# An attention layer's gate projection, moved behind the attention loop and done with seven block products for each pair of heads

## The chip, the cores and the metric

The kernel runs on one core of a Trainium2 chip. A core has TensorE (PE in the profile; its weight loads are PEld), VectorE (DVE), ScalarE (ACT), GpSimd (POOL) and SyncE (SP, which only issues DMAs here), an SBUF of 128 partitions, and a PSUM of eight banks into which TensorE accumulates. The metric is the device time of one execution in microseconds, the median of several runs.

## The reference

A trunk of two layers over 1024 latent tokens of width 1024, with a context prefix of 256 tokens. The first layer, which the change is about, is windowed attention with a gate:

```python
proj = h_lat @ w_in                                  # (1024, 1024) @ (1024, 5120)
q = apply_rope(split_heads(proj[..., :q_end], 16), cos, sin)       # 16 heads of 128
k = apply_rope(split_heads(proj[..., q_end:k_end], 4), cos, sin)   # 4 key heads
v = split_heads(proj[..., k_end:v_end], 4)
z = proj[..., v_end:]                                # the gate, 2048 wide
kv_c = h_ctx @ w_in[:, q_end:v_end]                  # keys, values of the context
...
o = windowed_attention(q, k, v, kc, vc, sink)        # |i-j| <= 128, all context keys, a sink logit
y = (o * jax.nn.silu(z)) @ w_out
...
x = x + gate * y
```

The second layer is a Conformer convolution with its own gate and output projection, and a final RMSNorm ends it. `h_lat` is the modulated norm of `x`. Everything is float32.

## The kernel before

**Products in three parts.** Each float32 operand of a product is split into a high part (rounded to TensorE's fp32r) and a low part (the rest). A product of 128x128 weights with 512 tokens is three matmuls: high by high, high by low, low by high (`mm3`, `gemm_half`). ScalarE makes the high part by a copy, VectorE or GpSimd the low part by a subtraction (`split_lo`). `Hh` and `Hl` are the high and low parts of `h_lat`, transposed: eight tiles of 128 channels by 1024 tokens.

**Stages.** The start computes the modulation, transposes `x` and projects the first key head, query head and value head. Then comes the attention loop over 128 steps `(h, qb)`: 16 heads, 8 blocks of 128 queries. Then the output projection (`proj_attn`), the convolution's input projection and convolution, and its output projection.

**A step of the attention loop.** `scores` issues six matmuls for the next step's queries against up to 384 window keys and 256 context keys; VectorE subtracts the mask and takes the maximum into `p_page`, ScalarE takes the exponent, VectorE the reciprocal, GpSimd scales. `transposes` turns the probabilities of this step (five 128x128 blocks) into PSUM, from which ScalarE makes `pthi` and VectorE `ptlo`. After four blocks `pv` multiplies them with V, multiplies by the gate and writes `ozd` in DRAM. Scores and transposes share a PSUM pair (`ps_s`, two buffers of two banks).

**Fill.** Between these TensorE works through `fillq`, a queue of projection jobs: `job(("q", n))` and `job(("z", n))`, 48 matmuls of 128x512 each. `fill(FILL)` takes twelve matmuls per step. The gate job ends in `finish`: `silu(z)` is formed as z(tanh(z/2)+1)/2 and stays in `zt` until `pv`. Every fourth head a new key head begins; its K and V jobs run in one piece between two steps.

**Other work in the loop.** `ada_rest` sums the modulation of the second layer row by row on VectorE (one call per step, accumulator in `mask_page`). `low_parts` splits the output weights of both layers once and puts the low halves into DRAM (`wolA`, `wolC`). In the last head the first seven rows of blocks of the output projection run early as fill (`early_proj`, EARLY_ROWS).

**Order.** `pin("P")` keeps TensorE's instructions in the order of the program; on the other engines and in SyncE's queue a scheduler orders them when the program is built. `after(...)` puts an operation behind the softmax's on its engine. SBUF beside the constants is 45 pages of 4 KB per partition (`pg`) and 6 half pages (`hp`); a page is handed out in the order in which pages were freed, and a write to it waits for the last reader.

## Time and profile before

| | |
|---|---|
| time, median of 3 runs | 1757.66 us (1756.83 to 1758.03) |
| profiled execution: span of its instructions | 1752.9 us |
| profiled execution: time of its own beside the span | none given by the page |
| attention loop, 110 to 850 us: VectorE, ScalarE, GpSimd busy | 416.1, 360.1, 403.4 us of 740 |
| HBM read, written | 188.70 MB, 41.69 MB |

The page lists each engine's busy time, the span in 40 slices, the chain of work that ended last, and groups of instructions. A group's line reads: source line, engine, operation, output<-inputs by the program's names, shapes, count, then busy time in us and the mean of one in ns, then the engine's idle time before them and what ended it. All instructions are issued through one helper, so that the source line is the same for all; groups are told apart by their tile names: `psg<-hh_page,whi_page` is a projection, `pss<-ident,p_page` the transposes, `p_page<-pss,mask_page,nsink` the masked maximum, `mask_page<-wsum_raw,...` and `dww_raw` the modulation sum, `wlo_page` a weight's low part, `low_page` the output weights' low halves. Matmuls overlap: a matmul's own duration is longer than the distance to the next.

### The profile page before, as it was taken

Reading aid. Unit: us, or ns where it says so; the run is one execution under the profiler, and the core shown is the slowest. Engines: PE = TensorE matmul, PEld = TensorE weight load, DVE = VectorE, ACT = ScalarE, POOL = GpSimd, SP = SyncE. Lnnn points to the kernel's source line nnn. Section 1 sums busy time; section 2 is a strip of 40 time slices with the busy share of each in tenths; the row PEclk is TensorE's granted clock in tenths of the full one; section 3 lists DMA queues with packets and bytes.
Section 4 is the critical chain, followed back from the end, with each engine's and each line's share of the span. In section 5 each row is a group of like instructions: output and inputs, shape, how many; then the busy total and the mean of one; then the engine's idle time right before and its main releaser. Section 6 shows DMA issues by size and latency. Waiting matters only on the chain.

```text
span 1752.9 us, 23877 instructions
## 1 busy us (share of the span) xinstructions
PE 1720.7 (98%) x8420; PEld 1424.8 (81%) x8420; DVE 1148.3 (66%) x2079; ACT 889.4 (51%) x1548; POOL 895.4 (51%) x705
## 2 busy tenths in 40 slices
PE   7999999999999999999999999999999999999997
PEld 4788888888888888888888888888888888788886
DVE  6755564556546563656315189999999999867823
ACT  7555553445345444545334355554665564466731
POOL 0245654566636565653101267998898888130300
PEclk9999999999999999999999999999999999999999
DMA  9334443444334542436777733011121202377971
GB/s 313 107 82 139 136 133 85 145 147 145 100 105 143 152 142 87 136 119 203 279 250 239 241 90 105 13 54 31 43 79 36 91 30 79 120 254 243 325 264 48
DMA packets 195324, 242.45 MB, mean 138 GB/s; under 512 B 11798, under 2 KB 126790, under 8 KB 195204
## 3 DMA queue, kind: packets, MB, share of 16 engines
q1 hardware_dynamic: 188516, 230.10, 40.3%
q10 hardware_dynamic: 6688, 10.83, 2.6%
q8 instruction: 66, 1.08, 0.3%
q14 instruction: 54, 0.44, 0.1%
HBM read 188.70 MB, written 41.69 MB: 131 GB/s over the span
## 4 chain that ended last, share of the span: by engine, by line
PE 86%; DMA 5%; DVE 3%; POOL 2%; ACT 2%; issue 2%; SPq 1%; ACTq 0%; POOLq 0%; DVEq 0%
PE psg L89 44%; PE pss L89 22%; PE pso L89 19%; DMA araw_page<-in_ada_w_dram 1%; POOL rope_half L89 1%; DMA low_page<-in_conv_w_out_dram 1%; DMA rope_half<-rope_half 1%; SPq L89 1%; DMA low_page<-in_attn_w_out_dram 1%; DMA wolC<-low_page 1%; DVE mask_page L89 1%; ACT p_page L89 0%; POOL wlo_page L89 0%; POOL low_page L89 0%; DMA wraw_page<-in_attn_w_in_dram 0%
## 5 line engine op out<-in xcount | busy, mean ns | idle before, releaser
L89 POOL TENSOR_TENSOR odd_half<-odd_half,prod_half 128x513 f32<-128x513 f32 (+2 forms) x252 | 312.8, 1250 | 24.2 <-ACT prod_half L89 11.0
L89 PE MATMUL psg<-hh_page,whi_page 128*128 128x512 f32 x600 | 237.6, 396 | 0.0
L89 PE MATMUL psg<-hh_page,wlo_page 128*128 128x512 f32 x600 | 236.9, 395 | 0.0
L89 PE MATMUL psg<-hl_page,whi_page 128*128 128x512 f32 x600 | 236.8, 395 | 0.0
L89 POOL TENSOR_TENSOR wlo_page<-wraw_page,whi_page 128x1024 fp32r<-128x1024 f32 x70 | 173.1, 2475 | 104.1 <-ACT whi_page L89 83.2
L89 ACT ACTIVATE prod_half<-ubuf,dww 128x513 f32<-128x513 f32 (+2 forms) x252 | 165.1, 674 | 107.3 <-POOL odd_half L89 105.1
L89 POOL TENSOR_SCALAR p_page<-p_page,sc 128x640 f32<-128x640 f32 (+1 forms) x128 | 100.8, 787 | 224.4 <-DVE sc L89 208.7
L89 PE MATMUL psg<-h2h_page,whi_page 128*128 128x512 f32 x464 | 183.9, 396 | 0.0
L89 PE MATMUL psg<-h2h_page,wlo_page 128*128 128x512 f32 x464 | 183.0, 394 | 0.0
L89 PE MATMUL psg<-h2l_page,whi_page 128*128 128x512 f32 x464 | 182.4, 393 | 0.0
L89 DVE SCALAR_TENSOR_TENSOR pss<-ubuf,dww,pss 128x512 f32<-128x512 f32 (+3 forms) x270 | 172.3, 670 | 0.1
L89 DVE SCALAR_TENSOR_TENSOR pss<-ubuf,wsum,pss 128x512 f32<-128x512 f32 (+3 forms) x270 | 171.7, 670 | 0.2
L89 DVE TENSOR_TENSOR ptlo<-pss,pthi 128x640 fp32r<-128x640 f32 (+1 forms) x144 | 103.3, 717 | 64.0 <-ACT pthi L89 62.8
L89 ACT ACTIVATE p_page<-p_page,sc 128x641 f32<-128x641 f32 (+1 forms) x128 | 102.7, 802 | 74.1 <-DVE sc L89 69.7
L89 ACT ACTIVATE pthi<-pss 128x640 fp32r<-128x640 f32 (+1 forms) x144 | 88.6, 615 | 91.7 <-PE pss L89 86.3
L89 PEld LDWEIGHTS psg<-hh_page,wlo_page 128*128 128x128 f32 x600 | 112.9, 188 | 26.3
L89 PEld LDWEIGHTS psg<-hh_page,whi_page 128*128 128x128 f32 x600 | 113.0, 188 | 20.8 <-DVE kvc_page L89 0.2
L89 PEld LDWEIGHTS psg<-hl_page,whi_page 128*128 128x128 f32 x600 | 112.9, 188 | 20.7
L89 ACT ACTIVATE whi_page<-wraw_page 128x1024 fp32r<-128x1024 f32 x88 | 92.6, 1053 | 69.0 <-PE psg L89 25.5
L89 PE MATMUL pso<-h2l_page,whi_page 128*128 128x512 f32 x304 | 119.9, 394 | 0.0
L89 PE MATMUL pso<-h2h_page,whi_page 128*128 128x512 f32 x304 | 119.8, 394 | 0.0
L89 PE MATMUL pso<-h2h_page,wlo_page 128*128 128x512 f32 x304 | 119.6, 394 | 0.0
(244 smaller groups left out, 4105.2 us busy)
## 6 DMA issues: line engine op xcount, KB each, us to landing
wraw_page<-in_conv_w_in_dram SPq DMA_DIRECT2D x48, 512.0 KB
wraw_page<-in_attn_w_in_dram SPq DMA_DIRECT2D x40, 512.0 KB
wol_page<-wolA SPq DMA_DIRECT2D x32, 512.0 KB
wo_page<-in_attn_w_out_dram SPq DMA_DIRECT2D x32, 512.0 KB
wo_page<-in_conv_w_out_dram SPq DMA_DIRECT2D x32, 512.0 KB
wol_page<-wolC SPq DMA_DIRECT2D x32, 512.0 KB
rope_half<-rope_half ACTq DMA_DIRECT2D x80, 128.0 KB
araw_page<-in_ada_w_dram SPq DMA_DIRECT2D x32, 256.0 KB
```

What stands on the lines that cost most here:

```text
L89: r = f(*a, **k)
```

## The change

Two heads' gate weights and the two halves of the tokens make a 2x2 by 2x2 block product over the two halves of the 1024 channels. The change computes it with seven block products in place of eight (Winograd's form). `t_prep` forms the four sums of activation blocks, a quarter of the channels in each of the heads 0, 4, 8 and 12, and stores them split in DRAM (`td`); `z_prep` forms the sums of weight blocks for each pair; `dense` issues the products and `z_evac` combines them. `pv` no longer gates: it stores the attention output in DRAM (`od`), and `z_out` reads it back, multiplies by the gate and writes `ozd`. The first pairs are fill of the last three heads, the others run behind the loop. Scores are issued two steps ahead, fill is five matmuls before the transposes and four or five behind them, K and V of the next key head are fill jobs that read the context's operands back from DRAM (`kept`), the early rows of the output projection are gone, and its low weight halves are made on GpSimd when needed (`wolA` is gone).

```diff
-FILL = 12
-EARLY_ROWS = 7
-EARLY_FROM = 3
...
+        after_q[h] = [("q", h + 2)] if h + 2 < NH else []
+        if g < NG and h % 4 == 1:
+            after_q[h].append(("k", g))
+        if g < NG and h % 4 == 3:
+            after_q[h].insert(0, ("v", g))
...
-        items = [... for w, d in ((Wo, wolA), (Wp, wolC)) for m in range(2) for kk in range(NK)]
+        items = [... for w, d in ((Wp, wolC),) for m in range(2) for kk in range(NK)]
...
+            split_lo(G, wl, w, wh)
...
-        stt(oz[:, 0:512], o, 0.5, zt[h][:, sl], ALU.mult, ALU.mult)
-        SY.dma_start(out=ozd[h, :, sl], in_=oz[:, 0:512])
+        act(oz[:, 0:512], o, AF.Copy)
+        SY.dma_start(out=od[h, :, half * 512:half * 512 + 512], in_=oz[:, 0:512])
...
+    def t_prep(k):
...
+        def v(out, p, q, op):
+            after(tt(V, out, p, q, op))
+        def g(out, p, q, op):
+            after(tt(G, out, p, q, op), anchor_p)
+        def out(n, t):
+            q = pg.alloc(F32R, [2, 512], "tq")
+            act(q[:, 0], t, AF.Copy)
+            after(split_lo(V, q[:, 1], t, q[:, 0]))
+            SY.dma_start(out=td[n, k], in_=low(q))
+            pg.free(q)
+        g(c, l11, l12, ALU.subtract)
+        v(a, h11, h12, ALU.subtract)
+        yield
+        v(a, a, c, ALU.add)
+        out(0, a)
...
+    def z_prep(g):
+        r1, r2 = zraw.pop(g)
+        z_pair(g, 0, r1, V)
+        yield
+        tt(G, s3, r1[:, 0:4], r2[:, 0:4], ALU.add)
+        tt(G, r2[:, 0:4], r2[:, 0:4], r2[:, 4:8], ALU.add)
+        yield
+        tt(G, r1[:, 0:4], r1[:, 0:4], r2[:, 0:4], ALU.add)
+        tt(G, r1[:, 4:8], r1[:, 4:8], r1[:, 0:4], ALU.add)
+        yield
+        z_pair(g, 1, r1, V)
...
+        z_pair(g, 2, r2, G)
...
+    PRODS = {"p1": (0, 0, "11"), "p2": (0, 4, "21"), "r6": (1, 0, "t2"), "p3": (1, 4, "22"),
+             "r5": (2, 0, "t1"), "r4": (2, 4, "t4"), "r7": (3, 0, "t3")}
...
+        if alone[0]:
+            t = s_alloc() if name == "p2" else c
+            act(t, c, AF.Silu)
+            tt(G, t, t, o, ALU.mult)
...
+                for k in range(4):
+                    rh, rl = xq(mv, k)
+                    for m, (w, x) in enumerate(((wh, rh), (wh, rl), (wl, rh))):
+                        PE.matmul(o, w[:, k0 + k], x, ...)
+                        yield
...
+        if tgen:
+            next(tgen, None)
+        if h >= NH - 3:
+            next(pgen, None)
+        elif lstate[0] == "open" or h % 4 == 0 and len(pg.free_) > 3:
             lstate[0] = next(lows, "shut")
...
-            scores(*nxt)
-            fill(15 if h and h % 4 == 0 and qb < 4 else FILL)
+            scores(*steps[i + 2])
+        fill(5)
         if pvq:
             pv(*pvq.popleft())
         transposes(h, qb)
+        fill(4 + qb % 2)
...
+    alone[0] = True
+    for v in zall:
+        if v == "starve":
+            next(pgen)
+        elif v is not None:
+            next(pgen, None)
+            next(pgen, None)
+            next(adag, None)
+            lstate[0] = next(lows, "shut")
```

## The prediction

> **What bounds the kernel now.** I read the head of the page and its slices first, to see which engine is full and where.

> ```profile
> span 1752.9 us, 23877 instructions
> PE 1720.7 (98%) x8420; PEld 1424.8 (81%) x8420; DVE 1148.3 (66%) x2079; ACT 889.4 (51%) x1548; POOL 895.4 (51%) x705
> ...
> PE   7999999999999999999999999999999999999997
> ...
> PEclk9999999999999999999999999999999999999999
> ```

> TensorE is busy in every slice but the first and the last, at full clock. A busy digit does not say that it is at its peak, so I looked next at the chain that ended last, for the distance between matmuls, and at TensorE's list of waits between 105 and 850 us, which is the attention loop.

> ```profile
> 292.41 3.47 PE pso L89 x21
> ...
> 977.41 44.47 PE pss L89 x192
> ...
> engine line waited for: us in total, times, longest us
> PE pss L89 <- DVE ptlo L89: 3.6, 2, 3.2
> PE pss L89 <- DVE sc L89: 1.3, 3, 0.9
> PE psg L89 <- DVE rope_half L89: 1.0, 1, 1.0
> PE pss L89 <- POOL p_page L89: 0.5, 1, 0.5
> ```

> 192 matmuls of 128x512 in 44.47 us are 0.2316 us each, without a gap. The loop of some 740 us holds only 3.6 + 1.3 + 1.0 + 0.5 = 6.4 us of waits. So this kernel is bound by the number of matmul columns, and any matmul taken out is worth its full 0.2316 us, as long as the other engines keep up.

> **What the change removes from TensorE.** Before, the gate projection is 16 heads x 2 halves x 24 matmuls = 768. After, each of 8 pairs has seven products of 4 x 3 matmuls: 8 x 84 = 672. The 96 that go are worth 96 x 0.2316 = **-22.2 us**. Nothing else changes in number: the Q, K, V, score, transpose, P·V and output matmuls are the same, and the 84 early output matmuls that filled the last head only move behind the loop, at the same price each. In the order of the built program two pairs (168 matmuls) run as fill in the last heads and six (504) alone behind the loop.

> The waits of the old loop belong to its order (scores one step ahead, K and V run in one piece between groups). With scores two steps ahead they go: **-6.4 us**; I charge the new order's own waits below.

> **The shorter step.** Fill per step falls from 12 to 9.5 matmuls (five, then four or five). The timeline of TensorE shows one old step:

> ```profile
> 396.45 0.40 PE L89 MATMUL psg<-hh_page,whi_page 128*128 128x512 f32 x1
> ...
> 399.26 0.71 PE L89 MATMUL pss<-ident,p_page 128*128 128x128 f32 x5
> 399.73 0.42 PE L89 MATMUL pss<-kh_page,qh_page 128*128 128x384 f32 x1
> ...
> 400.70 0.39 PE L89 MATMUL psg<-hh_page,whi_page 128*128 128x512 f32 x1
> ```

> Twelve fills take 2.81 us, five transposes 0.47, six score matmuls 0.97: 4.25 us. The new step is 4.25 - 2.5 x 0.2316 = 3.67 us; every fourth one also has the P·V block of 3.47 us. Four steps come to 3 x 3.67 + 7.14 = 18.2 us. That is still TensorE work, but the other engines now have to serve a step in 3.67 us where they had 4.25. So I listed what they do per step, between 280 and 840 us, VectorE's groups first, then GpSimd's and ScalarE's:

> ```profile
> L89 DVE CUSTOM_DVE_ANT_0 p_page<-pss,mask_page,nsink 128x640 f32<-128x640 f32 x72 | 63.1, 876 | 10.5 <-PE pss L89 10.1
> L89 DVE TENSOR_TENSOR ptlo<-pss,pthi 128x640 fp32r<-128x640 f32 x69 | 56.6, 820 | 31.4 <-ACT pthi L89 31.4
> L89 DVE SCALAR_TENSOR_TENSOR mask_page<-wsum_raw,cs,mask_page 128x256 f32<-128x256 f32 x47 | 38.3, 814 | 0.0
> L89 DVE TENSOR_TENSOR rope_half<-psg,cos_page 128x512 f32<-128x512 f32 x26 | 18.0, 691 | 32.0 <-ACT rope_half L89 24.9 <-POOL ql_page L89 5.8 <-issue 0.7
> L89 DVE RECIPROCAL sc<-sc 128x1 f32<-128x1 f32 x94 | 15.0, 160 | 64.0 <-ACT p_page L89 63.8
> L89 DVE TENSOR_TENSOR ozl_page<-ozf_page,ozh_page 128x1024 fp32r<-128x1024 f32 x6 | 7.3, 1223 | 4.7 <-ACT ozh_page L89 4.7
> ...
> L89 POOL TENSOR_TENSOR low_page<-low_page,lhi_half 128x512 f32<-128x512 f32 x50 | 65.4, 1308 | 0.0
> L89 POOL TENSOR_TENSOR wlo_page<-wraw_page,whi_page 128x1024 fp32r<-128x1024 f32 x26 | 63.5, 2445 | 20.1 <-ACT whi_page L89 19.1 <-POOL p_page L89 1.0
> L89 POOL TENSOR_SCALAR p_page<-p_page,sc 128x640 f32<-128x640 f32 x71 | 57.9, 815 | 116.0 <-DVE sc L89 109.0 <-DMA wol_page<-wolA 3.0 <-PE psg L89 2.9
> ...
> L89 ACT ACTIVATE p_page<-p_page,sc 128x641 f32<-128x641 f32 x71 | 58.8, 829 | 52.5 <-DVE sc L89 52.3
> L89 ACT ACTIVATE pthi<-pss 128x640 fp32r<-128x640 f32 x70 | 48.9, 698 | 48.7 <-PE pss L89 48.5
> ```

> A plain step costs VectorE 0.88 + 0.82 + 0.16 + 0.81 (the modulation sum, one per step) + a quarter of 0.69 (one half of Q's rotation every four steps) = 2.84 us, of 3.67. ScalarE has 0.83 + 0.70 for the softmax. Plain steps fit, and I charge **+1 us** for the occasional late one (the old loop paid 6.4 us over 128 steps).

> **The added preparation on VectorE.** In heads 0, 4, 8 and 12 each of ten steps also gets a piece of the preparation of the activation sums (t_prep): 11 VectorE operations on 128x512 and 5 on GpSimd for each of four tiles, in the same heads in which the low halves of the convolution's output weights go over GpSimd. Whether that fits hangs on one thing that the trace shows: a VectorE operation with both inputs in SBUF does not run beside a GpSimd one. The modulation sum's durations (minimum, median, maximum), and the two engines side by side:

> ```profile
> L89 DVE SCALAR_TENSOR_TENSOR mask_page<-wsum_raw,cs,mask_page x47: 472/485/2203, 304.0 to 824.6; 128x256 f32<-128x256 f32 x47
> ...
> 395.83 0.49 DVE L89 SCALAR_TENSOR_TENSOR mask_page<-dww_raw,cs,mask_page 128x256 f32<-128x256 f32 x1
> ...
> 398.79 2.10 DVE L89 SCALAR_TENSOR_TENSOR mask_page<-wsum_raw,cs,mask_page 128x256 f32<-128x256 f32 x1
> 400.82 0.15 DVE L89 RECIPROCAL sc<-sc 128x1 f32<-128x1 f32 x1
> 400.89 0.80 DVE L89 TENSOR_TENSOR ptlo<-pss,pthi 128x640 fp32r<-128x640 f32 x1
> ...
> 395.97 1.03 POOL L89 TENSOR_SCALAR p_page<-p_page,sc 128x640 f32<-128x640 f32 x1 [5.41 <-DVE sc L89]
> 396.96 1.30 POOL L89 TENSOR_TENSOR low_page<-low_page,lhi_half 128x512 f32<-128x512 f32 x1
> 398.21 2.40 POOL L89 TENSOR_TENSOR wlo_page<-wraw_page,whi_page 128x1024 fp32r<-128x1024 f32 x1
> ```

> The same sum takes 0.49 us alone and 2.10 us when it meets the weight split on GpSimd, and it ends 0.28 us after that split; the softmax split behind it starts late. In the mean it takes 0.814 us, 0.33 us of it waiting. [...]

> One t_prep operation I take at 0.69 us (the rotation's 128x512 row, the nearest in size) plus the wait. VectorE's step is then 2.51 us free (2.84 - 0.33) + 1.1 x 0.69 = 3.27 us, plus the wait on 2.1 operations. At the old mean of 0.33 us that is 3.96 us: four steps are 15.9 of TensorE's 18.2, but each of the three steps without P·V is 0.3 us too long. There is slack for that: from one transposes to the next TensorE has 3.67 - 0.47 = 3.2 us of other work, and the high and low split between them need 0.70 + 0.82, which leaves 1.7 us. So 0 us. The wait should be longer, though: in such a head of 36.4 us GpSimd has six rotation operations, five of t_prep and some five low halves of 1.31 us and one split of 2.45, 24 us, or 0.65 of the time, and a VectorE operation that meets one waits 0.9 us of it in the mean (half of 1.31 or more): 0.6 us. Then the step is 4.53 us, three steps are 2.6 us too long, and the P·V step gives that back to VectorE but not to TensorE. Over 10 such triples (4 tiles x 2.5) it is 26 us without the slack, and 10 x (2.6 - 1.7) = 9 us with it. Ends 0 and +26; I take **+9**.

> **The last head.** In the built order three steps of head 15 have no fill at all, since the second pair's operands are not yet issued. Such a step has 0.47 + 0.97 = 1.44 us for TensorE, and cannot be shorter than transposes, high split and low split in a row, 0.47 + 0.70 + 0.82 = 2.0 us and hops. Three times 0.7, and a wait for the second pair's product: **+3** (0 to 8: a weight split of 2.45 and an addition chain of 4 x 1.31 on GpSimd late by one step).

> **The stage behind the loop.** 6 x 84 matmuls and the rest of the second pair, some 560 x 0.2316 = 130 us. GpSimd has per pair 4 additions, 1 sum and 4 gate products of 1.31 us and a split of 2.45: 14.2 us of TensorE's 19.5; with 9 leftover low halves (11.8) and the first output-weight splits (4 x 2.45) it is 107 us. If every two-input VectorE operation (per pair two splits of 1.22, one of 0.69, seven sums of 0.49: 6.6 us) pushes it back, 146 us, which is 16 late. Pairs are prepared more than one ahead, and gate products may run late without TensorE noticing. Ends 0 and +16; **+4**.

> **The handover and the rest.** The output projection's low weight split moves from a DRAM copy (wolA) to GpSimd: 2.45 us per 24 matmuls of 5.56 us, beside TensorE. Cover is the pair before; if the first split is late it costs its 1.06 + 2.45 us. **+1** (0 to 4). The copies that go (wolA) and come (od, td, kept) stay off the path: TensorE did not wait for a DMA in the old loop. The convolution starts earlier, otherwise unchanged: 0.

> **Sum.** -22.2 - 6.4 + 1 + 9 + 3 + 4 + 1 = -10.6 us. The page gives no time of its own for the profiled execution beside its span of 1752.9 us; the runs' median is 1757.66, 4.8 us outside the span, which I keep. 1757.66 - 10.6 = **1747 us**.

> **Rivals.**
> *All of it is covered.* The waits turn out as in the old loop, with 2 us in all: 1757.66 - 28.6 + 2 = 1731. For it: VectorE's 15.9 us of 18.2. [...] Chance 0.24.
> [...] VectorE's steps in heads 0, 4, 8, 12 cost TensorE, and GpSimd, held out by VectorE, delays the pairs behind the loop. It decides from 28.6 us of stalls on; without the slack a mean wait of 0.45 us is enough, 30 x (3.27 + 2.1 x 0.45 - 3.67) = 16 us in the loop beside 8 behind it and the 5 of the rest. Upper ends: 26 + 16 + 1 + 3 + 1 = 47. Midway to the break-even point, 38: 1757.66 - 28.6 + 38 = 1767. For it: the rows above; against: GpSimd is 51% busy. Chance 0.25.
> *The pairs arrive late.* [...] Chance 0.09.
> That the change does not do what it says is not open: the built program has the 672 matmuls.

> **Numbers.** Forecast 1747, chance 0.42, itself from 1739 to 1755. What a measurement can tell from no change is 0.2%, 3.5 us: below 1754.1 is faster. Faster: 0.24 + 0.39 + 0.02 = 0.65. Same: 0.03 of the forecast, 0.05 of the late pairs, 0.02 of the lock: 0.10. Slower: 0.25. The range of 8 in 10 goes from 1731 (all covered) to 1769 (just past the lock's middle).

> **What would show it.** In the profile after, TensorE's list of waits between 105 us and the end of the loop should hold 10 to 16 us, most of it for ptlo and sc (VectorE) in heads 0, 4, 8 and 12; the preparation's operations (tx_page) should have a minimum near 0.69 us and a mean over 1; the stage behind the loop should last 130 to 136 us, with waits for zlo or zhi at pair borders. It is wrong if TensorE's matmul distance changes, if a DMA ends its waits, or if the waits sum to under 5 or over 30 us.

## The result and the profile after

| | before | after |
|---|---|---|
| time, median | 1757.24 us (1755.0 to 1758.03, 4 runs) | 1806.13 us (1801.96 to 1807.98, 4 runs) |
| span of the profiled execution | 1752.9 us | 1804.3 us |
| mean granted clock of TensorE | 0.996 | 0.986 |

The change makes the kernel slower by 2.8% (ratio 1.028, 95% interval 1.0264 to 1.0296). The forecast was 1747 us, faster, with a range up to 1769.

The head of the page after, with the slices of TensorE:

```profile
span 1804.3 us, 24082 instructions
...
PE 1723.9 (96%) x8324; PEld 1413.5 (78%) x8324; DVE 1228.5 (68%) x2120; ACT 917.1 (51%) x1597; POOL 1048.8 (58%) x784
...
PE   7989998999999998889899999999999999999997
```

TensorE has the 96 matmuls less that were counted (8420 before, 8324 now), but slices with 8 (each is 45 us) stand at the start of the loop, at 271 us, where head 4 begins, at the loop's end, in the new stage and at its border to the output projection. The starts of the transposes (minimum, median and maximum duration, then first and last start) give the loop's ends, before and after; the output projection's matmuls give the end of the new stage:

```profile
L89 PE MATMUL pss<-ident,p_page x608: 269/273/328, 110.4 to 849.0; 128*128 128x128 f32 x152
```

```profile
L86 PE MATMUL pss<-ident,p_page x608: 270/272/447, 111.6 to 719.2; 128*128 128x128 f32 x152
...
L86 PE MATMUL psg<-woh_page,ozh_page x96: 387/394/793, 880.3 to 1025.5; 128*128 128x512 f32 x96
```

Below, "the loop" is the time from the first to the last of these transposes (after: 719.2 - 111.6 = 607.6 us), "the stage" the time from there to the first output matmul (161.1 us). "Lost time" adds up, over all matmuls of a part, how much longer the distance to the next start was than it usually is for that matmul between the same neighbours; it holds the waits and the stretches at half clock (a granted clock of 0.50).

| part | lost before | lost after | difference |
|---|---|---|---|
| loop | 14.8 | 50.3 | +35.5 |
| stage behind it | - | 23.4 | +23.4 |
| output projection | 1.3 | 10.3 | +9.0 |
| start, convolution and the rest | 27.8 | 28.5 | +0.7 |

With -22.2 us for the 96 matmuls that is +46.4 us; the spans differ by 51.4, so 5.0 us are not placed. What TensorE waited for, in the loop and then in the stage:

```profile
engine line waited for: us in total, times, longest us
PE pss L86 <- DVE sc L86: 13.8, 12, 3.0
PE pss L86 <- DVE ptlo L86: 11.7, 8, 3.3
PE pss L86 <- POOL p_page L86: 5.8, 4, 2.7
PE pso L86 <- ACT pthi L86: 1.2, 2, 0.8
PE pso L86 <- DVE ptlo L86: 0.3, 1, 0.3
...
PE psg L86 <- DVE spare_pthi L86: 5.0, 1, 5.0
PE pss L86 <- DVE spare_pthi L86: 3.4, 3, 2.1
PE pss L86 <- DVE spare_ptlo L86: 3.1, 3, 1.9
PE pss L86 <- ACT spare_ptlo L86: 2.5, 1, 2.5
```

32.8 us in the loop where it was 6.4, for the same releasers, `sc` and `ptlo`: VectorE has not yet read a PSUM bank that TensorE needs next. In the stage too the waits are for banks that VectorE or ScalarE have not read out (`spare_...` are the tiles the products are read into), not for the pairs' weights `zhi` and `zlo`.

VectorE and GpSimd are not full in either part (columns TensorE, its weight loads, VectorE, ScalarE, GpSimd, clock, DMA share, GB/s):

```profile
105.00:719.00 614.00, 580.75 (x3338) 502.17 (x3337) 395.89 (x777) 324.44 (x722) 365.51 (x309) 0.99 0.45 141
719.00:880.00 161.00, 146.97 (x603) 114.55 (x603) 81.10 (x87) 54.10 (x77) 113.86 (x75) 0.95 0.63 205
```

How such a wait comes about shows in the timeline of head 0, VectorE first, then GpSimd, then TensorE:

```profile
122.10 1.78 DVE L86 TENSOR_TENSOR tx_page<-hh_page,hh_page 128x512 f32<-128x512 f32 x1
123.80 1.75 DVE L86 TENSOR_TENSOR tq_page<-tx_page,tq_page 128x512 fp32r<-128x512 f32 x1
125.47 0.87 DVE L86 CUSTOM_DVE_ANT_0 p_page<-pss,mask_page,nsink 128x640 f32<-128x640 f32 x1
...
121.87 1.46 POOL L86 TENSOR_TENSOR low_page<-low_page,lhi_half 128x512 f32<-128x512 f32 x1
123.29 1.71 POOL L86 TENSOR_TENSOR rope_half<-rope_half,rope_half 128x512 f32<-128x512 f32 x1
...
121.71 0.76 PE L86 MATMUL pss<-ident,p_page 128*128 128x128 f32 x5 [2.59 <-DVE ptlo L86]
...
126.41 0.44 PE L86 MATMUL pss<-kh_page,qh_page 128*128 128x384 f32 x1 [3.00 <-DVE sc L86]
```

Two t_prep operations with both inputs in SBUF take 1.78 and 1.75 us in place of 0.68 between 122.1 and 125.5 us, beside two GpSimd operations; the read of the scores' bank (125.47) stands behind them, and TensorE waits 3.00 us for that bank. GpSimd's two take 1.46 and 1.71 us, where each takes 1.29 in the median of the loop when no two-input VectorE operation is under way as it starts.

Of the 50 sums `acc_a<-wsum_raw` in the changed kernel between 105 and 690 us, 17 start while a two-input GpSimd operation is under way: 16 of them take 0.53 to 2.58 us and end 0.28 to 0.29 us after it, the last, which starts as it ends, takes 0.48. The 20 without any GpSimd operation beside them take 0.47 to 0.48. The expectations call this the lock, and what it adds to an operation lock time or lock wait.

### The profile page after: what moved, and what is told of

It reads as the page before. It is cut to its first block, busy times and chain, and to the rows that moved or that the text cites. A ratio compares the mean times of both kernels' runs of the same rounds, so it can differ in the third digit from the quotient of the medians.

```text
span 1804.3 us, 24082 instructions
## 1 busy us (share of the span) xinstructions
PE 1723.9 (96%) x8324; PEld 1413.5 (78%) x8324; DVE 1228.5 (68%) x2120; ACT 917.1 (51%) x1597; POOL 1048.8 (58%) x784
## 3 DMA queue, kind: packets, MB, share of 16 engines
q1 hardware_dynamic: 195684, 244.78, 41.4%
q8 instruction: 65, 1.06, 0.2%
## 4 chain that ended last, share of the span: by engine, by line
PE 71%; DMA 7%; DVE 5%; POOL 4%; issue 3%; ACT 2%; SPq 0%; ACTq 0%; POOLq 0%; DVEq 0%
PE psg L86 34%; PE pss L86 20%; PE pso L86 18%; DMA rope_half<-rope_half 2%; DVE acc_a L86 2%; POOL rope_half L86 1%; DMA zraw_page<-in_attn_w_in_dram 1%; POOL low_page L86 1%; DMA wolC<-low_page 1%; DMA ozf_page<-ozd 1%; DVE p_page L86 1%; POOL wlo_page L86 1%; ACT p_page L86 1%; DVE ptlo L86 1%; DMA wsum_raw<-in_ada_w_dram 1%
## 5 line engine op out<-in xcount | busy, mean ns | idle before, releaser
L86 POOL TENSOR_TENSOR odd_half<-odd_half,prod_half 128x513 f32<-128x513 f32 (+2 forms) x252 | 314.5, 1256 | 23.7 <-ACT prod_half L86 10.5
L86 POOL TENSOR_TENSOR wlo_page<-wraw_page,whi_page 128x1024 fp32r<-128x1024 f32 x54 | 134.2, 2485 | 71.5 <-ACT whi_page L86 57.2
L86 PE MATMUL psg<-hl_page,whi_page 128*128 128x512 f32 x344 | 140.2, 408 | 0.0
L86 PE MATMUL psg<-hh_page,wlo_page 128*128 128x512 f32 x344 | 139.9, 407 | 0.0
L86 PE MATMUL psg<-hh_page,whi_page 128*128 128x512 f32 x344 | 139.8, 406 | 0.0
L86 ACT ACTIVATE woh_page<-wo_page 128x1024 fp32r<-128x1024 f32 x64 | 67.4, 1055 | 113.3 <-DMA wo_page<-in_conv_w_out_dram 38.9
L86 PE MATMUL pss<-woh_page,gs_page 128*128 128x512 f32 x352 | 114.2, 394 | 0.0
L86 POOL TENSOR_TENSOR wol_page<-wo_page,woh_page 128x1024 fp32r<-128x1024 f32 x32 | 78.3, 2454 | 60.6 <-ACT woh_page L86 57.5
L86 DVE CUSTOM_DVE_ANT_0 p_page<-pss,mask_page,nsink 128x640 f32<-128x640 f32 (+1 forms) x112 | 96.0, 857 | 23.4 <-PE pss L86 12.2
L86 PE MATMUL pss<-ident,p_page 128*128 128x128 f32 x608 | 89.0, 276 | 21.4 <-DVE ptlo L86 11.7
```

The lines of the kernel that those rows point to most:

```text
L86: r = f(*a, **k)
```

## The experiments

Times are medians; the kernel before ran beside every group at 1755.1 to 1757.0 us. Loop and stage are from the profiled execution. In the loop, runs that change nothing there lie between 605.4 and 607.6 us. In the stage they lie between 156.6 and 163.0 us, so 4 us there prove little.

### What VectorE's side work costs: left out

The first theory was that VectorE's own order is too full: t_prep and the modulation sums stand in front of the reads of the banks.

Without t_prep's arithmetic (`e1_no_tprep`):

```diff
         def v(out, p, q, op):
-            after(tt(V, out, p, q, op))
+            pass
         def g(out, p, q, op):
-            after(tt(G, out, p, q, op), anchor_p)
+            pass
...
-            act(q[:, 0], t, AF.Copy)
-            after(split_lo(V, q[:, 1], t, q[:, 0]))
+            act(q[:, 0], h11, AF.Copy)
+            act(q[:, 1], l11, AF.Copy)
```

> Leaves out the arithmetic of t_prep (44 VectorE and 20 GpSimd operations on 128x512); ScalarE copies h into the same pages and the copies to td stay. In the changed kernel TensorE's matmul distances between 100 and 719 us hold 47 us more than their medians. Theory A (VectorE's operations with two SBUF inputs, held out by GpSimd's, come ahead of the softmax in VectorE's order; t_prep's are the larger half): this excess falls to some 15 us, the stage behind the loop stays as it is, time 1806 - 32 = 1774 us. Rival B (the step of 3.67 us is too short for the softmax chain whatever else VectorE has): the excess stays over 35 us, time above 1795 us.

Measured: 1787.41 us (ratio to before 1.0166, 1.014 to 1.0191), loop 593.9, stage 163.0. t_prep is worth 13.7 us of the loop: a part, not the larger half, and the time lies between the two expectations.

Without the modulation sums, loads kept (`e2_no_modsum`), and without both (`e4_neither`):

```diff
-                after(stt(acc_a, raw, cs[:, kt:kt + 1], acc_a, ALU.mult, ALU.add))
+                pass
```

> Leaves out the modulation sums behind the first tile of each column block (112 of 128 VectorE operations on acc_a); their loads stay. Theory A: 32 of VectorE's 67 us of lock time in the loop go with it, the loop's excess falls from 47 to some 20 us, and behind the loop, where these sums take 34 us of VectorE, some 5 of 37 us: time about 1774 us. Rival B: loop as it is, time above 1795 us.

> Leaves out both t_prep's arithmetic and the modulation sums. Theory A: the loop's excess falls to some 5 us, the time to 1806 - 42 - 5 = about 1759 us, close to the kernel before; what is left is the stage behind the loop. Rival B: over 35 us of excess stay in the loop, time above 1790 us.

Measured: 1806.30 and 1804.58 us. These two decide nothing. With nothing between them, each load waited in SyncE's queue for the one before it, and everything else in that queue behind it; in the second of them, between 100 and 250 us, the chain reads

```profile
by line: DMA wsum_raw<-in_ada_w_dram 52.2%; PE psg L86 20.2%; PE pss L86 13.1%; PE pso L86 9.8%; issue 1.1%; DMA gd<-acc_a 1.1%; POOL rope_half L86 0.9%; DVE acc_a L86 0.8%; ACT p_page L86 0.6%; DVE ptlo L86 0.5%; ACT pthi L86 0.3%; SPq L86
```

So they were repeated with the loads left out too (`e5_no_modsum_no_loads`, `e6_neither_no_loads`):

```diff
-            if i + 1 < len(todo):
+            if kt == KT - 1 and i + 1 < len(todo):
                 load(i + 1)
```

> Leaves out the modulation sums behind the first tile of each block and their loads too (with the loads kept but nothing between them, each waited on SyncE's queue for the one before, which put a new wait in front of everything else on that queue). Reference: in the changed kernel the loop from the first transposes to the last takes 607.6 us with 35 us of gaps between TensorE's matmuls, the stage from there to the output projection 161.1 us with 16, the projection 191.5 with 8. Theory A2 (t_prep and the modulation sums together fill VectorE in the loop; without t_prep the loop took 13.7 us less): the sums are worth about as much, loop 594 us; behind the loop the gaps at 793, 799 and 835 us end with sums and go, 6 us: time about 1785 us. Rival F (the sums are filler that waits its turn; the loop's rest is the last two heads without fill): loop over 603 us, time above 1797 us.

> Leaves out t_prep's arithmetic and the modulation sums with their loads. TensorE's order is that of the changed kernel. Theory A2: loop about 582 us (what stays are some 10 us of gaps in the last three heads and those at the start), stage behind it about 155 us, time 1806 - 26 - 6 = 1774 us. Rival F: loop as without t_prep alone (594 us), time 1785 us or more. Rival B (the short step itself is too short): also 594 us, with gaps that wait for sc and ptlo spread over all heads.

Measured: without the sums 1781.21 us (1.0143, 1.0126 to 1.0159), loop 595.3, stage 149.7; without both 1775.58 us (1.0106, 1.0088 to 1.0124), loop 585.5, stage 155.0. Both times are near theory A2's. The sums with their loads, which the change does not touch, cost 12 us of the loop and 6 to 11 of the stage (155.0 and 149.7 us in these two runs); with t_prep 22 us of the loop. But even so the kernel is 20 us slower than the kernel before beside it (1755.60 us).

### GpSimd's low halves left out

`e3_no_lows`:

```diff
-                after(split_lo(G, raw[:, b], raw[:, b], hi[:, 0:512]), anchor_p)
+                pass
```

> Leaves out GpSimd's subtraction for the low halves of the convolution's output weights (32 operations of 1.31 us on GpSimd, most of them in heads 0, 4, 8 and 12 beside t_prep, 9 or so behind the loop); loads, ScalarE copies and stores stay. Theory A: less of GpSimd's work to meet, the loop's excess falls from 47 to some 30 us. Theory C (behind the loop GpSimd's list is what is late): there the excess falls from 37 to some 25 us. Time about 1778 us with both, 1795 with only C. Rival B and a rival D (behind the loop the loads of the pairs' weights are late, not GpSimd): no change there.

Measured: 1796.40 us (1.0226, 1.021 to 1.0242), loop 605.5, stage 154.1. Theory C holds for the stage (-7 us, 12 were expected). In the loop the 17 us expected are 2, which is within what unchanged loops differ by: taking away one of GpSimd's lists does not give TensorE time back there.

### The work moved instead of left out

t_prep on every second step (`e8_spread`), and in addition on GpSimd for three tiles of four (`e9_tprep_gpsimd`):

```diff
-        if tgen:
+        if tgen and (qb % 2 == 0 or h >= 12):
             next(tgen, None)
```

```diff
         def v(out, p, q, op):
+            if k < 3:
+                return g(out, p, q, op)
             after(tt(V, out, p, q, op))
...
-            after(split_lo(V, q[:, 1], t, q[:, 0]))
+            if k < 3:
+                after(split_lo(G, q[:, 1], t, q[:, 0]), anchor_p)
+            else:
+                after(split_lo(V, q[:, 1], t, q[:, 0]))
```

> Whole computation. The pieces of t_prep for the first three tiles go to every second step instead of every step (heads 0 to 2, 4 to 6, 8 to 10), the fourth tile as in the changed kernel; TensorE's order is unchanged. Theory A2 (too much for VectorE in the same steps): three quarters of t_prep's 14 to 16 us in the loop shrink to a third, time about 1798 us. Rival H (each two-input operation costs its lock wait wherever it stands): no change, 1803 to 1808 us.

> Whole computation. All of t_prep's arithmetic for the first three tiles goes to GpSimd (48 operations of 1.3 us instead of 15; VectorE's 33 go), spread over every second step as before; the fourth tile as in the changed kernel. TensorE's order unchanged. Theory A3 (what costs TensorE is the time that VectorE's order is occupied, by the operations and their lock waits): most of t_prep's share in heads 0 to 11 goes, the loop falls from 605 to 595 us, time about 1792 us. Rival I (VectorE's remaining two-input operations meet more of GpSimd's, and the scaling of p waits on GpSimd behind t_prep): the loop stays at 603 us or grows, with more waits for p_page.

Measured: 1801.68 us (1.0262, 1.024 to 1.0284), loop 605.0; and 1802.77 us (1.0269, 1.0248 to 1.029), loop 607.8. Neither is separated from the change itself. Spread, heads 0, 4 and 8 fell from 47.1, 43.6 and 43.6 to 44.8, 41.4 and 40.2 us, and heads 1, 5 and 9, where the work now stood, rose from 37.4, 36.0 and 37.2 to 39.2, 38.5 and 39.8. In these two runs the cost follows the operations, whichever step and whichever of the two engines they are on: rivals H and I, though the waits for `p_page` did not grow as rival I had it (5.5 us, 5.8 in the change).

### Is it the shorter step?

t_prep added to the kernel before (`e13_before_tprep`: the function and its calls in heads 0, 4, 8, 12, nothing else), and the changed kernel with the old length of step (`e15_dummy`):

```diff
         ql = qb % 4
+        if 0 < h < NH - 2:
+            for _ in range(2 + qb % 2):
+                PE.matmul(tb[:, 0:512], Hh[0][:, 0:P], Hh[0][:, 0:512], start=True, stop=True)
```

> The kernel before, with t_prep added in heads 0, 4, 8 and 12 as in the changed kernel (its results are stored and not used); nothing else. In the kernel before a step has 12 matmuls of fill and takes 4.25 us without P.V, against 3.67 in the changed one, and the low halves of the output weights go over GpSimd in the same heads. Theory B2 (the shorter step is why t_prep costs anything): at most 4 us are added to the kernel before. Rival H (each two-input operation costs its lock wait wherever it stands): 12 to 16 us are added.

> The changed kernel with two or three matmuls of 128x512 added in each step of heads 1 to 13 just ahead of the transposes, into the bank that the transposes overwrite: the step has its old length of 4.25 us again. 13 x 20 = 260 matmuls more, 260 x 0.2316 = 60 us of TensorE. Theory B3 (the short step is why the other engines' delays reach TensorE): in heads 1 to 13 most of the gaps go, some 15 to 20 of 25 us, and the time grows by only 40 to 45 us, to about 1848 us. Theory K2 (the delays cost what they cost at any length): it grows by the full 60 us, to 1866 us.

Measured: the kernel before with t_prep takes 1762.78 us (1.0043, 1.0028 to 1.0059), 7.7 us more than beside it, between the two expectations and about half of t_prep's price in the changed kernel: heads 0, 4, 8 and 12 grew by 8.7 us here, and leaving t_prep out of the changed kernel gave 15.4 us back in them. With the old step length the time is 1859.61 us, 53.5 more than the change, where 40 to 45 or 60 were expected: nearer K2. By heads it splits: in the ten heads of 1 to 13 without t_prep 6.6 us of the loss went, in heads 4, 8 and 12 3 us came on top. The added matmuls write the very bank that the transposes wait for, so this run lengthens only the time in which VectorE may read the scores. The step's length is a part of it; how large a part stays open.

### GpSimd's operations as memsets

Every two-input GpSimd operation of the loop becomes a memset of the same output (`e14_memset`), then two or three of them in turn, so that GpSimd is as busy as in the change (`e17_memset_long`). VectorE's list is the same.

```diff
     def tt(eng, out, a, b, op):
+        if eng is G and nog[0]:
+            nms[0] += 1
+            for _ in range(2 + nms[0] % 2):
+                r = G.memset(out.bitcast(F32) if out.dtype == F32R else out, 0.0)
+            return r
         return eng.tensor_tensor(out=out, in0=a, in1=b, op=op)
```

> In the attention loop every GpSimd operation with two inputs (rotation, low halves of Q, K and the weights, t_prep's part, the low halves of the output weights) becomes a memset of the same output, which reads nothing; the scaling of p stays. So it leaves out that arithmetic; VectorE's list is unchanged. Theory J (the lock between VectorE and GpSimd stretches VectorE's operations, and that is what TensorE waits for): VectorE's sums on acc_a come down from 0.68 to some 0.5 us in the mean and t_prep's from 1.2 to 0.7, and the loop falls from 607.6 to 590 us or less, near the 585 without these operations. Rival K (what counts is that these operations stand in VectorE's order at all): they get shorter, but the loop stays over 600 us.

> As the run with memsets in the loop, but two or three memsets in turn for each operation: GpSimd is as busy as in the changed kernel (2.5 x 0.53 = 1.3 us for 128x512), and still reads nothing in them. Leaves out the same arithmetic. Theory J (the lock): the loop stays near the 576 us of the single memsets, at most 582, and VectorE's sums near 0.5 us. Rival O (GpSimd's time: rotation and the scaling of p come late behind its list): the loop goes back to 595 us or more, with waits for p_page and for the scores' operands.

Measured: 1771.28 us (1.0078, 1.006 to 1.0096) with a loop of 575.9 us, and 1770.47 us (1.0082, 1.0065 to 1.0098) with 577.5. The durations of the sums and of t_prep's operations (minimum, median, maximum in ns) between 105 and 690 us, in the changed kernel and then in the run with the longer memsets:

```profile
L86 DVE SCALAR_TENSOR_TENSOR acc_a<-wsum_raw,cs,acc_a x50: 469/477/2577, 121.6 to 655.8; 128x256 f32<-128x256 f32 x50
...
L86 DVE TENSOR_TENSOR tq_page<-tx_page,tq_page x12: 673/1650/1785, 123.8 to 616.7; 128x512 fp32r<-128x512 f32 x12
L86 DVE TENSOR_TENSOR tx_page<-tx_page,hh_page x8: 677/1410/1777, 137.1 to 607.2; 128x512 f32<-128x512 f32 x8
```

```profile
L86 DVE SCALAR_TENSOR_TENSOR acc_a<-wsum_raw,cs,acc_a x50: 468/476/989, 121.2 to 631.4; 128x256 f32<-128x256 f32 x50
...
L86 DVE TENSOR_TENSOR tq_page<-tx_page,tq_page x12: 666/683/719, 122.2 to 594.0; 128x512 fp32r<-128x512 f32 x12
L86 DVE TENSOR_TENSOR tx_page<-tx_page,hh_page x8: 671/684/735, 129.6 to 584.6; 128x512 f32<-128x512 f32 x8
```

and the engines' busy time in the same stretch of that run (columns as above):

```profile
105.00:690.00 585.00, 572.73 (x3342) 498.65 (x3342) 345.74 (x778) 324.26 (x722) 342.43 (x563) 1.00 0.48 148
```

GpSimd is 342 of 585 us busy (366 of 614 in the change), and still the medians of 1.65 and 1.41 us are back at 0.68, the loop loses 20.2 us in place of 50.3, and TensorE's waits in it are 12.0 us in place of 32.8. That is theory J: not GpSimd's busy time, but its two-input operations. With them in the loop t_prep's `tq_page` operations take 1.65 us in the median, with memsets, which have no input, 0.68. So it is shown that GpSimd's two-input operations stretch VectorE's. That all of the loop's 30 us come by that way is not: a memset does not wait for inputs either, and the scaling of `p` can slip between two short ones.

### The stage and the two ends

The sum zv + zu on VectorE (`e7_zsum_on_vector`), the last modulation sums moved into the output projection (`e12_defer`), GpSimd's two-input operations of the stage as memsets (`e18_stage_memset`, with the function of the last section, one memset each), and two edits at the ends (`e10_ends`):

```diff
-                        tt(G, zv[g], zv[g], zu[g], ALU.add)
+                        tt(V if mine else G, zv[g], zv[g], zu[g], ALU.add)
```

```diff
-            next(adag, None)
             lstate[0] = next(lows, "shut")
...
+        for _ in range(2 if s or kk > 2 else 0):
+            next(adag, None)
     run(projA)
```

```diff
-    fill(18)
+    fill(30)
...
+            if name == "p2" and g == NZ - 1:
+                V.tensor_copy(t, c)
+                c = t
             act(t, c, AF.Silu)
```

> Behind the loop the sum zv + zu (one operation on 128x512 for each of six pairs) goes from GpSimd to VectorE; nothing else. GpSimd takes its operations in order, and at 764, 788 and 807 us it waits 4.6 to 6.3 us for a load of the next pair's weights with such a sum behind it; the PSUM bank of r7 is only released after the sum. Theory G (GpSimd's order holds up the release of the bank): the stage's 23 us of gaps and half clock fall to some 12, time about 1795 us. Theory D (the pairs' weights are late as such, from pages and loads): TensorE waits for zhi or zlo instead, and the time stays within 3 us of 1806.

> Whole computation. The last four blocks of the modulation sums (those for the convolution's gate, needed only at the end) leave the stage behind the loop and run in the output projection, with loads into other buffers. Without any of these sums the stage took 149.6 instead of 161.1 us. Theory M (the sums and their loads stand in front of the releases of PSUM banks on VectorE): the stage takes about 150 us, the projection no longer than now, time about 1795 us. Rival N (what is late there is the chain of GpSimd and of the loads of the pairs; the gaps move to it): stage over 157 us.

> Loop as in the changed kernel; in the stage behind it GpSimd's two-input operations (additions and splits of the pairs' weights, zv + zu, gate products, low halves) become memsets of the same outputs. Leaves out that arithmetic. Theory G2 (there too GpSimd's list and the lock hold up the releases of PSUM banks): the stage falls from 161 to some 145 us, the gap of 5 us at the handover stays (a load of the output weights), time about 1790 us. Rival D2 (loads and pages of the pairs): stage over 155 us.

> Whole computation; two edits at the two ends. Before the first step 30 instead of 18 matmuls of fill run (12 move ahead of the loop), while K's second half and Q's are rotated for the scores that now run two steps ahead. And for the last pair's p2 VectorE copies the PSUM bank out ahead of ScalarE's Silu, since ScalarE stood 6.6 us waiting for a load of the output weights with that Silu behind it, and TensorE waited 4.9 us for the bank. Theory L (both are local waits of the order): head 0, 47 us against 37 of its neighbours, falls by 3 to 5 us, and the gap at 886 us goes (5 us, less what then waits for the output weights); the last head has 12 matmuls less to fill it, which costs up to 3: time about 1800 us. Rival: the waits only move, to the next product of those loads and chains: 1804 to 1808 us.

Measured: the sum moved, 1800.36 us (1.0266, 1.0237 to 1.0294), stage 156.7: not separated from the change. The modulation sums moved, 1799.24 us (1.025, 1.0232 to 1.0269), stage 150.1 as theory M had it, but 6 us came back in the projection (197.8 in place of 191.5). How such a sum reaches TensorE stands in the changed kernel's timeline, VectorE and then TensorE:

```profile
834.72 0.48 DVE L86 SCALAR_TENSOR_TENSOR acc_a<-wsum_raw,cs,acc_a 128x256 f32<-128x256 f32 x1 [1.72 <-DMA wsum_raw<-in_ada_w_dram]
835.12 0.68 DVE L86 TENSOR_TENSOR spare_ptlo<-pss,spare_ptlo 128x512 f32<-128x512 f32 x1
...
835.86 0.73 PE L86 MATMUL pss<-t_page,zhi_page 128*128 128x512 f32 x2 [1.95 <-DVE spare_ptlo L86]
```

VectorE waits 1.72 us for a load with the read of the bank behind it.

With memsets in the stage: 1788.02 us (1.0189, 1.0173 to 1.0204), stage 153.8, projection 182.5. The waits in the stage of that run:

```profile
PE pss L86 <- DVE spare_pthi L86: 10.3, 1, 10.3
PE psg L86 <- ACT spare_pthi L86: 0.7, 1, 0.7
```

But for 0.7 us the waits between the pairs are gone (theory G2). GpSimd's list is much shorter in that run too (44.76 us busy between 720 and 865 us, 113.86 of 161 in the change), so in the stage its length and what its operations add to VectorE's are not told apart. One wait of 10.3 us remains, at the handover at 865 us. In the change it is 4.7 us and lies behind the stage's end. There ScalarE stands before a load of the output weights with the read of a bank behind it:

```profile
882.17 1.06 ACT L86 ACTIVATE woh_page<-wo_page 128x1024 fp32r<-128x1024 f32 x1 [6.63 <-DMA wo_page<-in_attn_w_out_dram]
...
885.97 0.57 ACT L86 ACTIVATE spare_pthi<-psg 128x512 f32<-128x512 f32 x1
```

The edits at the ends gave nothing: 1809.90 us (1.0303, 1.0282 to 1.0324), not separated from the change. The read of that bank was ahead of the load now, and TensorE waited 6.6 us for the next one; head 0 gained 3 us that the start and head 4 gave back. The waits only moved.

### Together, and GpSimd's operations in halves

The repairs together (`e16_combined`: e7, e8, e12, and the low halves in heads 4k and 4k + 1), and the same with every two-input GpSimd operation of the loop issued in two halves (`e19_halves`):

```diff
-        elif lstate[0] == "open" or h % 4 == 0 and len(pg.free_) > 3:
+        elif lstate[0] == "open" or h % 4 < 2 and len(pg.free_) > 5:
```

```diff
+        n = out.shape[1]
+        if eng is G and halves[0] and n % 2 == 0:
+            r = None
+            for s in (slice(0, n // 2), slice(n // 2, n)):
+                r = eng.tensor_tensor(out=out[:, s], in0=a[:, s], in1=b[:, s], op=op)
+            return r
```

> Whole computation, with the repairs that gave something: the sum zv + zu on VectorE behind the loop, t_prep on every second step, the last four blocks of modulation sums in the output projection, and the low halves of the convolution's output weights in heads 4k and 4k + 1 instead of partly behind the loop. Singly the first three gave 6, 4 and 7 us, and leaving the low halves out of GpSimd's list gave 10. If they add up: 1806 - 24 = 1782 us. If they share the same waits: 1793 us. Under both it is slower than the kernel before.

> Whole computation: the combined repairs (1782.9 us), and each two-input GpSimd operation of the loop issued as two of half the width. Theory P (a VectorE operation waits for the rest of the GpSimd operation it meets): the mean wait halves, VectorE's sums on acc_a fall from 0.68 to some 0.58 us in the mean, the loop from 595 to 587 us, time about 1775 us. [...]

Measured: 1782.94 us (1.0145, 1.0125 to 1.0165), loop 595.4, stage 144.9: the repairs add up in the total, and the kernel is still 26 us slower than before. Part by part they do not: the loop fell by 12 us, where moving t_prep alone left it at 605.0 and moving the modulation sums alone at 605.4; the low halves were not moved alone, so what gave the rest is open. In halves 1786.70 us (1.018, 1.0154 to 1.0207), loop 599.5, where theory P had 1775 and 587. The sums fell from 692 to 656 ns in the mean where 580 were expected, and a rotation of GpSimd went from 1.34 to 2 x 0.80 us. No version tried beats the kernel before.

## Why the prediction was wrong, point by point

**The 22.2 us of matmuls** are there; at full clock the distance of two stayed 0.23 us.

**"The waits of the old loop go" (-6.4)** failed. The scores run two steps ahead, but there are still only two PSUM tiles in turn for scores and transposes, so each set of scores waits until VectorE has read the set before it, as in the old loop. The waits for `sc` and `ptlo` rose from 4.9 to 25.5 us.

Where the loop lost its time shows by heads (from the first transposes of a head to those of the next, in us; the forecast's head is two groups of four steps, 2 x 18.2 = 36.4):

| heads | forecast | change | without t_prep | without the sums | no low halves | GpSimd's two-input operations as memsets (`e14_memset`) |
|---|---|---|---|---|---|---|
| 0, 4, 8, 12 (with t_prep) | 145.6 + 9 | 176.0 | 160.6 | 167.1 | 169.6 | 154.5 |
| 1 to 3, 5 to 7, 9 to 11 | 327.6 | 335.3 | 336.1 | 331.6 | 336.0 | 329.3 |
| 13 to 15 | - | 96.3 | 97.2 | 96.6 | 99.9 | 92.2 |

**"Plain steps fit, +1"** was nearly right: the nine heads without t_prep took 7.7 us more than nine of the forecast's heads, about what the old loop's waits were.

**t_prep, +9 (0 to 26)** is the step of the loop that failed: the four heads with t_prep took 30.4 us more than four of the forecast's heads, over the upper end. The mechanism it named is right: 21.5 of these 30.4 us go with single memsets in place of GpSimd's two-input operations, 17.7 with the longer ones. The wait for each operation was not taken too small either: in these heads t_prep's VectorE operations took 1.19 us in the mean and the modulation sums 0.84, which is 0.50 and 0.36 us over their undisturbed 0.69 and 0.48, where 0.6 was taken. What failed is the slack of 1.7 us in three steps, which brought 26 us down to 9, and the reckoning with a mean step: even without slack the measured waits come to 30 x (3.27 + 1.1 x 0.50 + 0.36 - 3.67) = 15 us (an estimate), half of what was lost. TensorE stops for single late reads, such as the 2.59 and 3.00 us in head 0, and half clock can follow (0.50 from 126.96 to 130.37 us, behind the second).

t_prep is not alone in that price: left out by themselves, t_prep gives back 15.4 us in these heads, the modulation sums with their loads 8.9 and the low halves 6.4, and t_prep and the sums together only 13.6, so the shares cannot be added. The sums were in the old loop's steps too and were charged nothing here beyond their 0.81 us of a plain step; of the 12 us that they gave back in the loop 8.9 lie in these four heads. What exactly takes the cover away, the length of the step or its order (scores, five fills, transposes, fills), stays open: the longer step gave a mixed result.

What would show it came out as said for t_prep: a minimum near 0.69 us (0.67), medians up to 1.65 us, the waits mostly for `ptlo` and `sc`. But the waits in the loop are 32.8 us, over the 30 at which the prediction called itself wrong.

**The last head, +3 (0 to 8)**: in the run with the longer memsets, gaps of 1.4, 1.2 and 1.1 us are left there, 3.7 in all; in the change the gaps over 0.6 us from 612 us on (the end of head 12 and heads 13 to 15) add up to 11.5.

**The stage, +4 (0 to 16)**, failed too: 23.4 us lost. The sum there looked at whether GpSimd's list is shorter than TensorE's (107 of 130 us) and at waits for `zlo` and `zhi`. It is, by the row above: 113.86 of 161 us. What it left out is that a bank is only free when VectorE and ScalarE have read it, in an order in which other things wait for GpSimd and for loads.

**The handover, +1 (0 to 4)**: 9 us lost in the projection. Not the low split on GpSimd was late, but the load of the weights ahead of it, which the old kernel's early rows had behind them long before.

**Half clock** was not priced at all. By the granted clock TensorE ran at half pace (0.50) in nine stretches of 3.4 or 6.8 us in the loop, the stage and the handover. It was busy in them for 31.7 us, so some 16 us are lost (an estimate: half of that). Before, the clock was 1.00 from 105 to 1022 us.

**The rivals.** The one at 1767 us (0.25; "the lock" in the numbers), that VectorE and GpSimd hold each other out in both parts, comes nearest: in the loop the runs show the longer operations (1.65 us with GpSimd's two-input operations, 0.68 with memsets), in the stage they do not tell this from the length of GpSimd's list, and its price is half of what was lost. Its stalls went up to 47 us at the most; here they are 22.2 + 51.4 + 6.4 = 80. It looked in the loop at heads 0, 4, 8 and 12 only, and put the GpSimd of the whole kernel (51% busy) against itself, where the loop's is 365.51 of 614, 60%. "The pairs arrive late" did not happen: TensorE waited for neither `zhi` nor `zlo`, and the loads that reached it were those of the output weights and of the modulation sums. With memsets for GpSimd's two-input operations in both parts the change would be at 1806.1 - 35.6 - 18.1 = some 1752 us, an estimate from two separate runs that leave work out: even then hardly a gain.

## What to carry to other kernels

Work that hides in a loop is hidden by that loop's slack. When a change shortens the steps and adds work to some of them, charge again for everything that lives in those steps, not just for what is added, and do not count slack as cover before you have seen what TensorE waits for there. For a bank that TensorE needs next, ask who reads it, and what stands ahead of that read in that engine's order and what those things wait for. VectorE operations with two SBUF inputs and two-input GpSimd operations have to be counted against each other (here t_prep's `tq_page` took 1.65 us in the median, 0.68 with memsets); neither moving t_prep from one to the other nor cutting GpSimd's operations into halves helped.

## What the runs showed of the hardware

TensorE's pace after a gap, in the changed kernel's timeline of TensorE, and then stretches of 3.4 us around the two gaps (columns as above: length, TensorE, its weight loads, VectorE, ScalarE, GpSimd, clock, DMA share, GB/s):

```profile
122.55 0.40 PE L86 MATMUL psg<-hl_page,whi_page 128*128 128x512 f32 x1
122.78 0.40 PE L86 MATMUL psg<-hh_page,wlo_page 128*128 128x512 f32 x1
...
837.27 0.63 PE L86 MATMUL pss<-t_page,zlo_page 128*128 128x512 f32 x1
837.70 1.05 PE L86 MATMUL pss<-t_page,zhi_page 128*128 128x512 f32 x2
```

```profile
116.80:120.20 3.40, 2.33 (x13) 1.71 (x11) 3.40 (x3) 1.35 (x3) 3.40 (x3) 1.00 0.16 40
120.20:123.60 3.40, 1.70 (x9) 1.18 (x9) 3.40 (x5) 0.79 (x2) 3.01 (x4) 1.00 0.08 20
123.60:127.00 3.40, 0.59 (x4) 0.59 (x5) 3.40 (x5) 0.61 (x1) 1.40 (x1) 0.99 0.23 92
...
833.50:836.90 3.40, 1.45 (x7) 0.87 (x6) 2.18 (x4) 1.06 (x3) 0.35 (x1) 1.00 0.10 35
836.90:840.30 3.40, 3.40 (x9) 2.26 (x7) 0.63 (x2) 1.52 (x3) 3.40 (x3) 0.50 0.21 77
```
